# Eight chunks of the second layer's first gate part multiplied right behind the first layer's last product

## The chip, the cores and the metric

The kernel runs on one core of one Trainium2 chip. The metric is the device time of one execution in microseconds. The kernel before was run three times; its profile is that of one further execution. Engine names: PE is TensorE, DVE is VectorE, ACT is ScalarE, POOL is GpSimd, SP is SyncE.

## The reference

One inference step of a trunk of two layers over 128 context tokens and 128 latent tokens, width 2048, in fp32. Cut to what matters here:

```
for l in range(2):
    mod = silu(c) @ w_mod[l] + b_mod[l]            # 2048 x 6144 per layer, two conditioning vectors
    shift, scale, gate = split(mod, 3)
    h = rms_norm(x, norm_w[l]) * (1 + scale) + shift
    columns = h @ w_in[l]                          # q, i, ff, fb, g, attention, S5, merge gates
    o_hg = hgrn2_both_directions(...)              # gated linear recurrence, 8 heads
    o_at = attention(...)
    o_s5 = s5_both_directions(...)                 # complex diagonal scan, then GLU
    merged = g_hg*(o_hg @ w_br[0]) + g_at*(o_at @ w_br[1]) + g_s5*(o_s5 @ w_br[2])
    x = x + gate * (merged @ w_out[l])
y = rms_norm(x, final_norm)
```

The modulation vector is computed in six parts of 1024 columns for each layer. Parts 0 to 3 hold shift and scale, parts 4 and 5 the gate, which is needed only at the very end of its layer.

## The kernel before

**The products.** Every large product goes through `gemm` (line 160): an output group is 512 columns wide, for both token sets (s = 0, 1), so it holds two banks of the PSUM pool `pg` (four banks). A weight piece `raw` (256 rows by 512 columns, 512 KB) is loaded by SP; ACT rounds each half of it to `wh` (line 138), DVE forms the remainder `wl` (line 139), and TensorE does six matmuls for a half: lines 178, 179 and 180 for each s. `raw`, `wh` and `wl` have four buffers each. A `in_group` or `w_out` group is 16 halves, 96 products; a `w_br` group is 8 halves, 48 products. There are 8064 such products, 4032 in each layer. In layer two the product numbered 5760 from the program's start is the last one of the first merge gate, and the next one is the first of the first branch's `w_br`, which multiplies `oh` and `ol`, the transposed output of the HGRN mixer.

**The side work.** `mod_part` (line 245) is a generator that loads 128 x 2048 chunks `wm` of `w_mod` (1 MB each, 256 rows of it), multiplies them by the conditioning vectors, 16 matmuls of 32 x 256 for each two chunks ("a burst"; the profile counts 32 rows for it), and adds the bias `bm`. Its `plan` names the PSUM pool, how many chunks accumulate in one bank, and how many make a burst. The parts of the gate use pool `m`: before the change the plan is `("m", 2, 2)` four times, so a bank is taken for one burst and given back after its `tensor_add`. `side_work` (line 141) advances the generator at a given rate at each weight piece; in layer one the parts 4 and 5 of layer one and 0 to 3 of layer two run there, in layer two the generator `gates` with layer two's parts 4 and 5.

**The small matmuls.** Pool `m` (`pm`, line 73, two banks of 128 x 512) also serves everything that the mixers need between the products: `transpose4` (tiles `tr`), the attention's `trq`, `trk`, `sc`, `ao`, and the HGRN unit's `lv`, `o`, `kt`, `st`. Pool `b` (two banks) serves the S5 mixer (`bt`, `cb`, `bu`, `yp`).

**The HGRN unit** (`hgrn_unit`, line 449) runs for each token set and each half of the heads, the two token sets in turn. It goes through seven levels. At each one ACT copies `mix` (line 488), TensorE multiplies `lv` into a bank of pool `m` (line 492), DVE merges the bank into `A` by a predicated copy (line 494), and DVE multiplies `Z` by decay factors (line 508, twice). After the seven levels comes `o` (lines 525 to 528), its norm (lines 530 to 536 and `rstd`), for s = 0 also `kt`, `kts`, `st`, `sts` (lines 540 to 550), then the product with the SiLU gate (line 1003) and the transposes for the branch.

**The S5 scan** (lines 889 to 895) is a loop of 64 steps of four small DVE operations for each quarter of the groups; it has lower priority on DVE than the HGRN unit.

**The end of a layer** (from line 1071): four groups of `w_out`; after the fourth DVE forms x, ACT its squares, `token_rstd` the norm, then `normed` (line 371) scales x into `xn` (line 382), TensorE transposes it, and DVE and ACT form `hf`, `hh`, `hl`, the left factors of the next layer.

**What sets the order.** A scheduler with priorities writes the instruction order of each engine when the kernel is built; on the chip each engine then executes its list in order. A matmul in TensorE's list that waits holds up every one behind it.

Of the kernel before, what the change touches and what calls it, by code (L numbers as in the profile page):

```python
# [22 lines left out]
L = 2  # L23
# [5 lines left out]
MB = 2  # L29
# [4 lines left out]
MTAGS = ((("k4", "q4"), 1), (("k4", "q4"), 1), (("k4", "k4"), 1))  # L34
# [20 lines left out]
P_PE = 6_000_000  # L55
# [6 lines left out]
class Builder:  # L62
# [74 lines left out]
    def split_from(self, src, hi, lo):  # L137
        self.nc.scalar.copy(hi, src)  # L138
        self.nc.vector.tensor_sub(lo, src, hi.bitcast(F32))  # L139

    def side_work(self):
        if self.side is not None:
            self.side_credit += self.side_rate
            while self.side_credit >= 1:
                self.side_credit -= 1
                if next(self.side, None) is None:
                    self.side = None
                    break
# [7 lines left out]
    def start_side(self, gen, rate):  # L156
        self.finish_side()
        self.side, self.side_rate, self.side_credit = gen, rate, 0.0

    def gemm(self, pieces, hi, lo, nk):  # L160

        nc = self.nc
        ps = [self.pg.tile([128, 512], F32, tag="g", name=self.nm("g")) for _ in range(2)]
        for kk, src in enumerate(pieces):
            self.side_work()
            with self.prio(P_TOP):
                raw = self.wp.tile([128, 2, 512], F32, tag="raw", name=self.nm("raw"), bufs=RAW)
                nc.sync.dma_start(raw, src.rearrange("p (a b) -> p a b", a=2))
            for j in range(2):
                with self.prio(P_TOP):  # L170
                    wh = self.wp.tile([128, 512], F32R, tag="wh", name=self.nm("wh"))
                    wl = self.wp.tile([128, 512], F32R, tag="wl", name=self.nm("wl"))
                    self.split_from(raw[:, j], wh, wl)
                k = 2 * kk + j
                with self.prio(P_PE):
                    for s in range(2):
                        sl = slice(s * 128, s * 128 + 128)
                        nc.tensor.matmul(ps[s], lo(k)[:, sl], wh, start=(k == 0), stop=False)  # L178
                        nc.tensor.matmul(ps[s], hi(k)[:, sl], wh, start=False, stop=False)  # L179
                        nc.tensor.matmul(ps[s], hi(k)[:, sl], wl, start=False, stop=(k == nk - 1))  # L180
        return ps

    def rstd(self, ssq, n, width):
# [61 lines left out]
    def mod_part(self, l, part, prio, tags, plan):  # L245
# [5 lines left out]
        nc, io = self.nc, self.io  # L251
# [4 lines left out]
        kb = 0  # L256
        for bank, run, burst in plan:
            apart = burst > 1
            ps = None
            for k0 in range(kb, kb + run, burst):  # L260
                ws = []
                for k in range(k0, k0 + burst):
                    with self.prio(P_TOP):
                        tag, n = next(tags)
                        for i in range(0, 2, n):
                            w = self.t(tag if isinstance(tag, str) else tag[i], "wm", (128, n * 1024))
                            nc.sync.dma_start(w, io["w_mod"][l, part, k][:, i * 1024:(i + n) * 1024])
                            ws += [w[:, j * 1024:(j + 1) * 1024] for j in range(n)]
                    if apart:
                        yield True  # L270
                with self.prio(prio):
                    if ps is None:
                        pool = dict(g=self.pg, m=self.pm, b=self.pb)[bank]
                        ps = pool.tile([128, 512], F32, tag=bank, name=self.nm("mod"))
                    for j, k in enumerate(reversed(range(2 * k0, 2 * (k0 + burst)))):
                        for i in range(4):
                            with self.prio(P_MIX if j + i else prio):
                                nc.tensor.matmul(ps[32 * i:32 * i + 32, 0:256], self.cT[:, 2 * k:2 * k + 32],  # L278
                                                 ws[k - 2 * k0][:, i * 256:i * 256 + 256], start=(k0 == kb and j == 0),
                                                 stop=(k0 + burst == kb + run and j == 2 * burst - 1),  # L280
                                                 tile_position=(0, 32 * i))
                    if k0 + burst == kb + run:
                        nc.vector.tensor_add(bm, bm, ps[:, 0:256])
                if k0 + burst < 8:
                    yield True
            kb += run
# [634 lines left out]
    def layer(self, l, x, rs):  # L921
# [144 lines left out]
        if l + 1 == L:  # L1066
            fn = self.t("ys", "fn", (128, D))
            src = io["final_norm"]
            with self.prio(P_PREP):
                nc.gpsimd.dma_start(fn, bass.AP(src.tensor, src.offset, [[0, 128], [1, D]]))  # L1070
        for n in range(4):
            ps = self.gemm([io["w_out"][l, n, kk] for kk in range(8)],
                           lambda k: mt[2 * (k // 8)][:, k % 8], lambda k: mt[2 * (k // 8) + 1][:, k % 8], 16)
            sl = slice(n * 512, n * 512 + 512)
            if n == 3:
                self.finish_side()
                with self.prio(P_CHAIN):
                    nc.scalar.activation(self.ts("warm", (128, 1)), self.eye32[:, 0:1], AF.Sqrt)
            for s in range(2):
                with self.prio(P_LAST if n == 3 else P_TOP):  # L1080
                    gb = self.t2("gb")
                    nc.gpsimd.dma_start(gb, bass.AP(self.gate_d.tensor, self.gate_d.offset + (l * 2 + s) * D + n * 512,
                                                    [[0, 128], [1, 512]]))
                    xr = self.t2("xr")
                    nc.gpsimd.dma_start(xr, (io["x"] if l == 0 else self.x_d)[s][:, sl])
                    nc.vector.tensor_mul(gb, gb, ps[s])
                    nc.vector.tensor_add(xn[s][:, sl], gb, xr)
                    if l + 1 < L:
                        nc.gpsimd.dma_start(self.x_d[s][:, sl], xn[s][:, sl])
                    self.square(ssq, xn, s, n)  # L1090
                if l + 1 == L:
                    with self.prio(P_TOP + 500_000):
                        nc.vector.tensor_mul(xn[s][:, sl], xn[s][:, sl], fn[:, sl])
# [49 lines left out]
    def build(self):  # L1143
# [19 lines left out]
            pass  # L1163
        with self.prio(P_PREP):
            self.setup()
        for l in range(L):
            x, rs = self.layer(l, x, rs)
            if l + 1 < L:
                def gates():
                    tags = itertools.cycle(MTAGS)  # L1170
                    for p in (4, 5):
                        yield from self.mod_part(L - 1, p, P_PE, tags, [("m", MB, MB)] * (8 // MB))

                self.gates = gates()
        with self.prio(P_TOP):
            self.final(x, rs)

# [106 lines left out]
```

## Time and profile before

| | |
|---|---|
| runs (us) | 2308.33, 2309.62, 2308.81; median 2308.81 |
| profiled execution | 2313.16 us, span 2311.1 us |
| PE | 2252.0 us busy, 97% of the span, 13320 instructions |
| DVE | 1817.3 us busy, 79% |
| ACT | 1191.2 us busy, 52% |
| mean granted TensorE clock | 0.992 |
| chain that ended last | PE 84%, DVE 3%, DMA 3% |

The share of an engine is the union of its instructions over the span. PE's rows overlap their neighbours, since matmuls are pipelined: the rate is read from the distance between starts, and a wait from the idle time in brackets behind a row.

### The profile page before, as it was taken

How to read it: one execution, taken by the hardware profiler on the slowest of the kernel's cores; microseconds unless marked ns; L12 is line 12 of the kernel's file. 1: busy time of each engine (PE TensorE's matmuls, PEld its weight loads, DVE VectorE, ACT ScalarE, POOL GpSimd, SP SyncE). 2: the span in 40 equal slices, each digit the busy share in tenths (PEclk: the TensorE clock that was granted, in tenths of full speed). 3: DMA queues.
4: the chain of work that ended last, by engine and by line, in shares of the span. 5: the costliest groups of instructions: out<-in, count | busy, mean ns of one | idle time of the engine just before them, and what ended most of it. 6: DMA issues, size and time to landing. Idle time of an engine off the chain costs nothing.

```text
span 2311.1 us, 38488 instructions
## 1 busy us (share of the span) xinstructions
PE 2252.0 (97%) x13320; PEld 1818.5 (79%) x13320; DVE 1817.3 (79%) x4863; ACT 1191.2 (52%) x2064; POOL 133.8 (6%) x245
## 2 busy tenths in 40 slices
PE   6999999999999999999989999999999999999997
PEld 4668888888887777877767888888888877888886
DVE  4987799889869779875575898899959958956565
ACT  4436655555454354544447565555564544555454
POOL 2000000100100100000010001000010010000000
PEclk8999999999999999999999999999999999999999
DMA  9975454345548869588764554344546667656765
GB/s 377 362 288 170 145 181 155 123 134 195 186 159 282 316 212 326 198 274 284 270 233 137 177 175 151 127 166 152 190 148 196 200 207 266 200 175 224 241 202 171
DMA packets 131363, 483.87 MB, mean 209 GB/s; under 512 B 17200, under 2 KB 17808, under 8 KB 126688
## 3 DMA queue, kind: packets, MB, share of 16 engines
q1 hardware_dynamic: 120960, 456.38, 58.0%
q0 software_dynamic: 9488, 23.97, 3.4%
q8 instruction: 104, 1.70, 0.3%
q10 hardware_dynamic: 720, 1.07, 0.1%
q14 instruction: 91, 0.75, 0.1%
HBM read 474.36 MB, written 6.98 MB: 208 GB/s over the span
## 4 chain that ended last, share of the span: by engine, by line
PE 84%; DVE 3%; DMA 3%; issue 1%; ACT 1%; POOL 0%; SPq 0%; DVEq 0%; POOLq 0%; ACTq 0%
PE g L178 24%; PE g L180 24%; PE g L179 23%; PE bu L877 3%; PE lv L492 2%; PE mod L278 2%; PE tr L134 2%; DMA wm<-w_mod 1%; PE yp L908 1%; DVE wl L139 1%; DMA bm<-b_mod 1%; DMA gate_d<-bm 1%; PE bt L795 1%; PE yp L901 1%; PE ao L632 0%
## 5 line engine op out<-in xcount | busy, mean ns | idle before, releaser
L138 ACT CAST wh<-raw 128x512 fp32r<-128x512 f32 x1344 | 828.3, 623 | 900.9 <-PE g L179 599.0
L139 DVE TENSOR_TENSOR wl<-raw,wh 128x512 fp32r<-128x512 f32 x1344 | 914.2, 687 | 285.5 <-ACT wh L138 260.1
L178 PE MATMUL g<-wh,hl 128*128 128x512 f32 x1984 | 784.4, 395 | 6.7 <-DVE hl L139 5.6
L179 PE MATMUL g<-wh,hh 128*128 128x512 f32 x1984 | 778.0, 392 | 0.0
L180 PE MATMUL g<-wl,hh 128*128 128x512 f32 x1984 | 698.7, 398 | 1.5 <-DVE wl L139 1.2
L178 PEld LDWEIGHTS g<-wh,hl 128*128 128x128 f32 x1984 | 373.6, 188 | 96.3 <-DVE hl L139 7.7
L179 PEld LDWEIGHTS g<-wh,hh 128*128 128x128 f32 x1984 | 373.7, 188 | 77.0 <-issue 1.0
L180 PEld LDWEIGHTS g<-wl,hh 128*128 128x128 f32 x1984 | 366.4, 188 | 84.0 <-DVE wl L139 4.7
L889 DVE TENSOR_TENSOR p<-s5sc,Sb 128x64 f32<-128x64 f32 x512 | 140.1, 274 | 16.8 <-ACT Sb L881 7.2
L178 PE MATMUL g<-wh,ol 128*128 128x512 f32 x384 | 151.3, 394 | 0.0
L179 PE MATMUL g<-wh,oh 128*128 128x512 f32 x384 | 150.0, 391 | 0.0
L895 DVE TENSOR_TENSOR Sb<-Sb,p 128x64 f32<-128x64 f32 x512 | 140.9, 275 | 9.0
L891 DVE TENSOR_TENSOR p<-s5sc,Sb 128x64 f32<-128x64 f32 x512 | 138.3, 270 | 0.0
L180 PE MATMUL g<-wl,oh 128*128 128x512 f32 x384 | 130.6, 394 | 0.8 <-DVE wl L139 0.8
L894 DVE TENSOR_TENSOR p<-p,p 128x64 f32<-128x64 f32 x512 | 112.7, 220 | 6.0
L179 PE MATMUL g<-wh,mt 128*128 128x512 f32 x256 | 99.8, 390 | 0.0
L178 PE MATMUL g<-wh,mt 128*128 128x512 f32 x256 | 99.6, 389 | 0.0
L278 PE MATMUL mod<-wm,cs 128*32 128x256 f32 x1408 | 90.1, 388 | 7.1 <-DMA wm<-w_mod 6.9
L178 PEld LDWEIGHTS g<-wh,ol 128*128 128x128 f32 x384 | 72.1, 188 | 16.8 <-issue 0.8
L180 PEld LDWEIGHTS g<-wl,oh 128*128 128x128 f32 x384 | 71.3, 188 | 17.7 <-DVE wl L139 2.1
L179 PEld LDWEIGHTS g<-wh,oh 128*128 128x128 f32 x384 | 72.1, 188 | 14.9
L180 PE MATMUL g<-wl,mt 128*128 128x512 f32 x256 | 83.1, 392 | 0.0
(325 smaller groups left out, 2116.7 us busy)
## 6 DMA issues: line engine op xcount, KB each, us to landing
raw<-w_in SPq DMA_DIRECT2D x496, 512.0 KB, 4.2
wm<-w_mod SPq DMA_DIRECT2D x128, 512.0 KB, 7.9
raw<-w_br SPq DMA_DIRECT2D x96, 512.0 KB, 4.2
wm<-w_mod SPq DMA_DIRECT2D x32, 1024.0 KB, 10.5
raw<-w_out SPq DMA_DIRECT2D x64, 512.0 KB, 4.4
raw<-w_glu SPq DMA_DIRECT2D x16, 512.0 KB, 4.3
gb<-gate_d POOLq DMA_DIRECT2D x16, 256.0 KB, 6.4
x<-x SPq DMA_DIRECT2D x2, 1024.0 KB, 6.9
```

Source lines behind the costliest of these rows:

```text
L134: nc.tensor.transpose(ps[:, k], src[:, k * 128:(k + 1) * 128], self.ident)
L138: self.nc.scalar.copy(hi, src)
L139: self.nc.vector.tensor_sub(lo, src, hi.bitcast(F32))
L178: nc.tensor.matmul(ps[s], lo(k)[:, sl], wh, start=(k == 0), stop=False)
L179: nc.tensor.matmul(ps[s], hi(k)[:, sl], wh, start=False, stop=False)
L180: nc.tensor.matmul(ps[s], hi(k)[:, sl], wl, start=False, stop=(k == nk - 1))
L278: nc.tensor.matmul(ps[32 * i:32 * i + 32, 0:256], self.cT[:, 2 * k:2 * k + 32], ws[k - 2 * k0][:, i * 256:i * 256 + 256], start=(k0 == kb ...
L877: nc.tensor.matmul(pps[x][:, j2, k], Bl[pr, d, ri, k, j2, :], U2[pr, j2, 2 * qh + k].rearrange("p s t -> p (s t)"), start=True, stop=True, ...
L889: tt(p0.rearrange("p d (j s) -> p d j s", s=2), view(sc, qd * 32, [[16, 2], [1, 16], [0, 2]]), view(Sb, i, [[ds, 2], [2 * W, 16], [W, 2]]) ...
L891: tt(p1, view(sc, 128 + qd * 64, [[32, 2], [16, 2], [1, 16]]), view(Sb, i + RI, [[ds, 2], [-RI, 2], [W, 16]]), ALU.mult)
L894: tt(p0, p0, p1, ALU.add)
L895: tt(cur, cur, p0, ALU.add)
```

## The change

`gates` is created once, in `build`, and layer one takes its first steps: the generator is advanced at three places of layer one's `w_out` stage, so that the first two chunks of layer two's part 4 are loaded during the third and fourth group, and four chunks (in the change's title eight, of 128 rows each) are multiplied behind the fourth group's last product. `last_product` records that product, and `behind` adds an order edge from it to each of the 32 matmuls. The rest of layer one's side work is finished before the third group and no longer before the end of the fourth. The first two chunks now take buffers `H8`, and the plan of the gate parts is `("m", 8, 2)` once: all eight chunks of a part accumulate in one bank of pool `m`.

```diff
+    def ahead(self, n):
+
+        for _ in range(n):
+            next(self.gates)
...
+    def behind(self, ins, prev):
+
+        if prev:
+            self.tc.add_manual_dep(ins.ins, prev.ins.name, mybir.DependencyInfo(
+                mybir.DependencyClass.NoSync, mybir.DependencyReason.DATA), reason="order")
+        return ins
...
-                        nc.tensor.matmul(ps[s], hi(k)[:, sl], wl, start=False, stop=(k == nk - 1))
+                        self.last_product = nc.tensor.matmul(ps[s], hi(k)[:, sl], wl, start=False, stop=(k == nk - 1))
...
         for n in range(4):
+            if n > 1 and l + 1 < L:
+                if n == 2:
+                    self.finish_side()
+                self.ahead(1)
             ps = self.gemm([io["w_out"][l, n, kk] for kk in range(8)],
...
             if n == 3:
+                if l + 1 < L:
+                    self.mod_after = self.last_product
+                    self.ahead(1)
+                    for _ in range(MB):
+                        self.ahead(1)
+                    self.ahead(1)
+                    self.mod_after = None
                 self.finish_side()
...
+        def gates():
+            tags = itertools.chain((("H8", 2), ("H8", 2)), itertools.cycle(MTAGS))
+            for p in (4, 5):
+                yield from self.mod_part(L - 1, p, P_PE, tags, [("m", 8, MB)])
...
-                        yield from self.mod_part(L - 1, p, P_PE, tags, [("m", MB, MB)] * (8 // MB))
```

**What moves on the engines.** The first place is PE's list at the end of layer one; `mod` is the modulation's bank, `wm` a chunk, `tr` the transpose of the next layer's `xn`. Before:

```order
L178 MATMUL g_12946<-wh_13113,mt_11306 128x512
L179 MATMUL g_12946<-wh_13113,mt_11305 128x512
L180 MATMUL g_12945<-wl_13114,mt_11305 128x512
L180 MATMUL g_12946<-wl_13114,mt_11305 128x512
L134 MATMUL tr_13160<-ident,xn_13158 128x128 x4
L134 MATMUL tr_13174<-ident,xn_13172 128x128 x4
L178 MATMUL g_13279<-wh_13283,hl_13157 128x512
```

Changed:

```order
L192 MATMUL g_12951<-wl_13120,mt_11305 128x512
L192 MATMUL g_12952<-wl_13120,mt_11305 128x512
L290 MATMUL mod_13129<-wm_12949,cs 32x256 x8
L290 MATMUL mod_13129<-wm_12751,cs 32x256 x8
L290 MATMUL mod_13129<-wm_13152,cs 32x256 x4
L290 MATMUL mod_13129<-wm_13150,cs 32x256 x4
L290 MATMUL mod_13129<-wm_13148,cs 32x256 x4
L290 MATMUL mod_13129<-wm_13146,cs 32x256 x4
L134 MATMUL tr_13207<-ident,xn_13205 128x128 x4
L134 MATMUL tr_13221<-ident,xn_13219 128x128 x4
```

Two bursts, 32 matmuls, now stand between layer one's last product and the first transpose of layer two. All go to one tile, `mod_13129`, whose later bursts stand behind products 6312 and 6358 of layer two; part 5's four bursts follow behind products 6396 to 6526.

The second place is PE's list in layer two, where the first gate ends and the first branch begins (behind product 5760). Before, `g_19819` being the gate and `g_20000` the branch:

```order
L180 MATMUL g_19818<-wl_19987,hh_13214 128x512
L178 MATMUL g_19819<-wh_19986,hl_13215 128x512
L179 MATMUL g_19819<-wh_19986,hh_13214 128x512
L180 MATMUL g_19819<-wl_19987,hh_13214 128x512
L178 MATMUL g_20000<-wh_20004,ol_19781 128x512
L179 MATMUL g_20000<-wh_20004,oh_19780 128x512
```

Changed, from the gate's last product on (`lv`, `o`, `kt`, `st` are HGRN's second half of the heads):

```order
L192 MATMUL g_19866<-wl_20034,hh_13261 128x512
L505 MATMUL lv_18938<-Z_18794,mix_18795 128x128 x4
L505 MATMUL lv_18948<-Z_18785,mix_18786 128x128 x4
L505 MATMUL lv_18958<-Z_18794,mix_18795 128x128 x4
L505 MATMUL lv_18968<-Z_18785,mix_18786 128x128 x4
L505 MATMUL lv_18978<-Z_18794,mix_18795 128x128 x4
L505 MATMUL lv_18988<-Z_18785,mix_18786 128x128 x4
L505 MATMUL lv_18997<-Z_18794,mix_18795 128x128 x4
L538 MATMUL o_19005<-i_18781,A_18849 128x128 x4
L555 MATMUL kt_19028<-ident,Z_18785 128x128 x4
L560 MATMUL st_19035<-i_18781,kts_19033 128x128 x4
L538 MATMUL o_19043<-i_18782,A_18857 128x128
```

Before, the last `lv` stood behind product 5476 and the last `st` and the transposes of `q` behind products 5544 to 5596, each with products in front of and behind it. Now seven `lv` of four matmuls, `o` (4 and 12), two `kt`, two `st` (4 each) and two `tr` (4 each) stand between product 5760 and product 5761 with no product among them; two more `tr` follow behind product 5772.

The third place is DVE's list in the same stretch of the changed kernel (`p` and `Sb` are the S5 scan's; `A` and `Z` the HGRN unit's):

```order
L507 COPY_PREDICATED A_18849<-msk,lv_18948 128x512
L521 TENSOR_TENSOR Z_18785<-Z_18785,T_18856 128x2x16x16 x2
L907 TENSOR_TENSOR p_3978_17047<-p_3978_17047,p_3979_17048 128x64
L908 TENSOR_TENSOR Sb_16829<-Sb_16829,p_3978_17047 128x2x32
L902 TENSOR_TENSOR p_3980_17053<-s5sc_1236,Sb_16829 128x64
L904 TENSOR_TENSOR p_3981_17054<-s5sc_1236,Sb_16829 128x64
L907 TENSOR_TENSOR p_3980_17053<-p_3980_17053,p_3981_17054 128x64
L507 COPY_PREDICATED A_18857<-msk,lv_18958 128x512
L521 TENSOR_TENSOR Z_18794<-Z_18794,T_18864 128x2x16x16 x2
L908 TENSOR_TENSOR Sb_16829<-Sb_16829,p_3980_17053 128x2x32
```

The third quarter of the S5 scan, which before began behind product 5754, has moved ahead into this stretch: DVE's list alternates between the HGRN unit's remaining levels and scan steps. From the merge of the first of the seven `lv` to the split of the first transpose for the branch (`ol`) it holds 23 scan steps, 6 further predicated copies, 14 multiplications of `Z`, 8 operations of 128 x 512 of the norms and gates, and 12 small ones.

On SP the two `H8` chunks (1 MB each) now stand behind the first `w_out` piece, four loads of 512 KB follow behind the third group's pieces, and the 4 MB are gone from layer two.

## Rows read from the trace of the kernel before

**Rows 1.** Engine windows of layer two: from HGRN's start, its middle, behind product 5760.

```profile
core 0: us, PE busy (x) PEld busy (x) DVE busy (x) ACT busy (x) POOL busy (x), PEclk, DMA share, GB/s
1418.00:1722.00 304.00, 303.68 (x1971) 256.18 (x1970) 263.15 (x688) 169.62 (x288) 21.92 (x36) 1.00 0.47 155
1480.00:1680.00 200.00, 200.00 (x1170) 170.88 (x1170) 188.58 (x520) 109.60 (x184) 7.06 (x11) 1.00 0.49 164
1722.00:1848.00 126.00, 126.00 (x568) 104.01 (x570) 118.84 (x355) 64.02 (x105) 0.00 (x0) 1.00 0.59 190
```

**Rows 2.** PE's timeline between the layers: start, length, what, count, idle before it.

```profile
1201.54 0.63 PE L180 MATMUL g<-wl,mt 128*128 128x512 f32 x2
1208.43 1.09 PE L134 MATMUL tr<-ident,xn 128*128 128x128 f32 x4 [6.27 <-DVE xn L382]
1211.47 1.09 PE L134 MATMUL tr<-ident,xn 128*128 128x128 f32 x4 [1.95 <-DVE xn L382]
...
1212.95 0.63 PE L179 MATMUL g<-wh,hh 128*128 128x512 f32 x1
1213.38 0.63 PE L180 MATMUL g<-wl,hh 128*128 128x512 f32 x1
```

**Rows 3.** Engine windows of the same stretch, for the granted clock (the column PEclk).

```profile
1202.00:1208.00 6.00, 0.17 (x1) 0.00 (x0) 4.72 (x14) 1.89 (x6) 1.10 (x2) 0.72 0.88 263
1208.00:1213.00 5.00, 2.62 (x10) 1.98 (x11) 3.14 (x8) 0.97 (x2) 0.00 (x0) 0.50 0.20 82
```

**Rows 4.** PE's timeline in layer two at one burst of the gate part.

```profile
2131.20 1.93 PE L278 MATMUL mod<-wm,cs 128*32 128x256 f32 x32
2133.06 0.73 PE L180 MATMUL g<-wl,oh 128*128 128x512 f32 x2
```

**Rows 5.** PE's timeline in HGRN's second half: `lv` in both banks, `st`, `o`, transposes.

```profile
1595.67 1.95 PE L492 MATMUL lv<-Z,mix 128*128 128x128 f32 x16
...
1645.54 1.05 PE L547 MATMUL st<-i,kts 128*128 128x128 f32 x8
1646.43 0.39 PE L525 MATMUL o<-i,A 128*128 128x128 f32 x2
...
1649.57 0.60 PE L542 MATMUL kt<-ident,Z 128*128 128x128 f32 x4
1649.93 0.49 PE L178 MATMUL g<-wh,hl 128*128 128x512 f32 x1
```

**Rows 6.** DVE's timeline in HGRN's second half: one scan step alone, then steps interleaved.

```profile
1633.05 0.28 DVE L889 TENSOR_TENSOR p<-s5sc,Sb 128x64 f32<-128x64 f32 x1
...
1633.99 0.69 DVE L139 TENSOR_TENSOR wl<-raw,wh 128x512 fp32r<-128x512 f32 x1
...
1637.60 0.27 DVE L895 TENSOR_TENSOR Sb<-Sb,p 128x64 f32<-128x64 f32 x1
1637.77 0.67 DVE L534 TENSOR_REDUCE ssq<-sq 128x4 f32<-128x512 f32 x1
1638.37 0.26 DVE L889 TENSOR_TENSOR p<-s5sc,Sb 128x64 f32<-128x64 f32 x1
...
1638.73 0.68 DVE L139 TENSOR_TENSOR wl<-raw,wh 128x512 fp32r<-128x512 f32 x1
...
1639.41 0.21 DVE L894 TENSOR_TENSOR p<-p,p 128x64 f32<-128x64 f32 x1
1639.54 0.68 DVE L139 TENSOR_TENSOR wl<-raw,wh 128x512 fp32r<-128x512 f32 x1
```

**Rows 7.** DVE's timeline at one level: predicated copy and two multiplications of `Z`.

```profile
1614.82 0.74 DVE L494 COPY_PREDICATED A<-msk,lv 128x512 f32<-128x512 uint8 x1
1615.44 1.29 DVE L508 TENSOR_TENSOR Z<-Z,T 128x512 f32<-128x512 f32 x2
```

**Rows 8.** Engine windows of layer one's last 115 us, and PE's wait there.

```profile
1088.00:1203.00 115.00, 111.83 (x581) 87.56 (x579) 69.19 (x120) 52.59 (x92) 13.14 (x22) 0.99 0.78 268
...
PE mod L278 <- DMA wm<-w_mod: 2.3, 1, 2.3
```

More of the change, by code (lines that the diff above doesn't have):

```diff
@@ L277, in mod_part @@
                             with self.prio(P_MIX if j + i else prio):
[L278 to L281, printed above, removed]
+                                self.behind(nc.tensor.matmul(
+                                    ps[32 * i:32 * i + 32, 0:256], self.cT[:, 2 * k:2 * k + 32],
+                                    ws[k - 2 * k0][:, i * 256:i * 256 + 256], start=(k0 == kb and j == 0),
+                                    stop=(k0 + burst == kb + run and j == 2 * burst - 1),
+                                    tile_position=(0, 32 * i)), self.mod_after)
                     if k0 + burst == kb + run:
@@ L1165, in build @@
             self.setup()
+        self.mod_after = None
+        def gates():
+            tags = itertools.chain((("H8", 2), ("H8", 2)), itertools.cycle(MTAGS))
+            for p in (4, 5):
+                yield from self.mod_part(L - 1, p, P_PE, tags, [("m", 8, MB)])
+        self.gates = gates()
         for l in range(L):
             x, rs = self.layer(l, x, rs)
[L1168 to L1171, printed above, removed]
-                        yield from self.mod_part(L - 1, p, P_PE, tags, [("m", MB, MB)] * (8 // MB))
-                self.gates = gates()
         with self.prio(P_TOP):
```

## The prediction

> **What bounds the kernel now.** I read the engine windows of layer two first, then TensorE's timeline between the layers, then the timelines of HGRN's second half, and against them the instruction order of both kernels. The windows [rows 1] show TensorE busy in all 126 us behind product 5760: 568 matmuls, 0.222 us each, the distance at which products follow each other at the full clock, so nothing holds TensorE there. From HGRN's start up to that product it is busy in 303.68 of 304 us, and DVE in 263.15. So a matmul taken out of this stream is worth its own time, and a matmul that fills an idle TensorE costs nothing. The one idle place of any size lies between the layers [rows 2]: behind the last product TensorE waits 6.27 us until the first transpose may start, then 1.95 us more.
>
> **What the change gains.** Two bursts leave layer two's stream. One burst takes 1.86 us there, from its start to that of the next product [rows 4], so the two are worth 3.7 us. Between the layers they need the same 3.7 us of a wait of 6.27 us whose end is set by DVE (the scaled x), so they fit, if their chunks have landed by then. A second gain comes with it: in the wait the granted clock falls, to 0.50 in the next 5 us, which is the 1.2 GHz level [rows 3]; a product then takes 0.43 us, from start to start [rows 2], and the two groups of four transposes last 1.09 us each against 0.60 us for four at 2.4 GHz [rows 2, 5]. If the bursts keep the clock up, the transposes alone give back 1.0 us and the first five products about 1 us. The engine still idles some 2.5 us behind them, so I take 1.0, with 0 and 2 as ends.
>
> **What the change costs in loads.** 4.2 MB more have to come within layer one's last 115 us. The transfers there are busy in 0.78 of the time at 268 GB/s [rows 8], that is 344 GB/s while busy, so 4.2 MB are 12.2 us and 25 us are free. But 2.5 MB of it (7.3 us) stand on SP's queue among the loads of the remaining side work, for which TensorE already waits 2.3 us once [rows 8]; behind SP's issue of the two `H8` chunks stand two `w_out` pieces and four side loads. I take 1 us, with 0 and 7.3 as ends. The two chunks in `H8` and the 1 MB pairs in the small buffers are read right behind the last product, and the second half of `hh` and `hl`, which needs the `H8` buffers next, is written more than 5 us later; I cost that at nothing. Finishing the side work at the third group moves no burst by more than 10 products; nothing. Fewer `tensor_add` of `bm` on DVE: nothing on the path.
>
> **What the change costs in PSUM.** This is the large term, and the diff hides it in the plan. With `("m", 8, 2)` the bank taken between the layers is given back only after part 4's last burst, behind product 6358. Pool `m` has two banks, so all of layer two's transposes, attention and HGRN matmuls share one. Before, the two token sets' `lv` stand side by side, 16 rows within 1.95 us [rows 5], one bank each; now each `lv` has to wait until DVE has merged the one before. The instruction order shows the result: in the changed kernel the levels of HGRN's second half come about 24 products apart for each `lv`, not for each pair, and seven of them, both `o`, both `kt`, both `st` and two transposes are left over when product 5760 is done. The next product is the first branch's, which needs the output of all of that, and TensorE keeps its order. So TensorE waits out a chain.
>
> Its length, from DVE's order between the first of these merges and the first split for the branch. Predicated copies: 6 by 0.62 us, from the start of one to that of the next operation [rows 7], 3.7. Multiplications of `Z`: 14, two in 1.29 us with a last tail of 0.08, so 0.60 each [rows 7], 8.4. Norm and gate operations: 8 by 0.60, as the reduction [rows 6], 4.8. Twelve small ones: not above the 0.17 us of the short operation in [rows 6], 2.0. Scan steps, which stand in DVE's list between them and can't be passed: 23. One alone takes 0.94 us (four operations, 1633.05 to 1633.99); interleaved with others its parts take 0.17 + 0.36 + 0.13 = 0.66 [rows 6]. That is 15.2 to 21.6 us; most steps in the list are cut by an HGRN operation, so I take 0.75 each, 17.3. Sum 36.2 us, ends 34.1 and 40.5. Ahead of it come the first `lv`, 0.9 us, and its merge, 0.6, behind it the split, 0.6: 38 us, ends 36 and 43, from product 5760 to product 5761.
>
> TensorE works in that time, and this work is no longer in the stream ahead. Four matmuls of `lv` or `st` take 0.89 us (`st` to `o` in [rows 5]); seven `lv` 6.2, two `st` 1.8, 16 of `o` at the same rate 3.6. Four transposes take 0.36 (`kt` to the product behind it, [rows 5]): two `kt` and four `tr` 2.2. Together 13.8 us, which I subtract. The clock adds something: TensorE has work in little over a third of the wait, and [rows 3] show the 1.2 GHz level after 6 us without any, so the 13.8 us may double. Only where DVE stands waiting for TensorE does that count (mainly the 12 matmuls of `o` for the latent tokens and the chain behind them); 3 us, ends 0 and 13.8.
>
> Elsewhere with one bank I count 2 us (0 to 10): the projections `i` of the second half are evacuated later, so the following gate groups find two accumulator banks instead of four and can't start before the previous group is evacuated.
>
> **The sum.** 38 - 13.8 + 3 + 2 + 1 - 3.7 - 1 = +25.5 us. On the profiled execution's 2313.16 us that is 2338.7; the median of the runs is 4.35 us (0.19%) lower, so 2334.
>
> A rule of the Trainium skill speaks against the change too, and more strongly. [Rows 7] show a merge of 0.62 us, and [rows 5] products of TensorE between the small matmuls, so a busy bank costs nothing as long as products stand behind the waiting `lv`. The Trainium skill (Perfetto Trace Analysis, Optimizing Tensor Performance, Matmuls) says that independent groups of matmuls should rotate through different banks, so that one's evacuation overlaps the next one's matmuls. By that rule alone every small group of layer two would pay, not only the ones left at the end. No run so far shows a single bank.
>
> **The rivals.**
>
> *DVE sets the pace, and the order costs nothing (not slower).* In the middle of HGRN DVE is busy in 188.58 of 200 us, and behind product 5760 in 118.84 of 126 [rows 1]. If DVE bound both stretches, it would not matter which of its work comes first: the scan steps done during the wait, and some 11 ahead of it, are missing behind product 5760, 34 by 0.75 = 25 us, and would be given back there. The result would be the gains alone, 2308.8 - 4.7 = 2304 us, or 2305 with the 1 us of the loads. It decides from the point at which DVE holds the products behind 5760 apart. Against it: they come 0.222 us apart, TensorE's own rate, so nothing can be given back there. Chance 0.10, half of it faster and half unchanged.
>
> *One bank costs everywhere (slower).* From HGRN's start each of 32 `lv` waits for a merge, 0.62 us and the way to it and back. If TensorE's order has no slack there, each exposes about 0.7 us (an estimate: the 0.62 us of [rows 7] and a tenth): 22 us more, 2356. For it: the order places each `lv` as soon as the bank is expected free. Against it: between two of them stand 24 products, 5.4 us. The page's rule above would lead here. Chance 0.13.
>
> *The loads are late, so the change does not do what it says (slower).* If the last pair of chunks lands after the last product, the burst waits on TensorE, and the transposes of layer two are queued behind it, so each microsecond counts in full; or the side work waits the whole 7.3 us earlier. Price up to 7 us, 2341. Against it: 25 us of free transfer time. Chance 0.12.
>
> *The forecast:* 0.65.
>
> **How the numbers follow.** The likeliest case gives 2334. Its low end takes the wait at 36, no cold clock, no other loss and the full gains: +16.5, less some relief of DVE ahead of product 5760 (11 scan steps come in, 8.2 us, about 19 us of HGRN go out), so 2316. Its high end takes 43 us and half of the cold clock's 13.8, and the second rival is at 2356, so 2358. That leaves out the first rival and the far tail, less than 0.2. A measurement of this kernel can tell about 0.2%, 4.6 us, from no change: faster 0.05, unchanged 0.05, slower 0.90.
>
> **What would show it.** In the changed profile: the two bursts between about 1202 and 1206 us with the first transpose not later than before; a single idle stretch of TensorE between the first gate and the first branch of layer two, with `lv` about 2.7 us apart and DVE nearly full of `Z`, `A` and scan steps; from there on the same rate as before. I am wrong if products stand between those `lv`, if the wait is below 20 us, or if the stream ahead of it shortens by much more than 13.8 us.

## The result, and the profile after

The changed kernel takes 2350.99 us (median of four runs, 2346.93 to 2351.41), the kernel before 2308.57 us in the runs beside it: a ratio of 1.0172, 95% interval 1.016 to 1.0184, or 42.4 us more. The forecast was 2334 us, slower, with a range of 2316 to 2358. Its sign was right, and so was the place of most of the loss; the loss was two thirds larger than the 25.2 us forecast (2334 less 2308.81).

The profiled execution of the changed kernel took 2351.36 us. From its page, the span and the first section (engine, busy time, share, instructions):

```profile
span 2349.6 us, 38463 instructions
...
PE 2269.6 (97%) x13320; PEld 1831.4 (78%) x13320; DVE 1822.0 (78%) x4857; ACT 1197.3 (51%) x2068; POOL 133.9 (6%) x245
```

The share of TensorE is what it was, 97%: a share over the whole span hides a wait of 2% of it, the more so since TensorE works, slowly, in most of that wait. The engine windows show it (columns as in [rows 1]). From HGRN's start to product 5760, the wait behind it, and what follows:

```profile
1416.00:1715.00 299.00, 293.66 (x1847) 244.16 (x1846) 250.87 (x674) 160.38 (x273) 20.80 (x38) 0.99 0.42 145
1722.00:1765.00 43.00, 26.89 (x114) 23.00 (x113) 39.27 (x138) 10.57 (x19) 1.60 (x2) 0.58 0.20 73
1768.00:1890.00 122.00, 120.31 (x738) 98.13 (x738) 93.33 (x251) 61.84 (x101) 7.77 (x16) 0.99 0.46 158
```

In the 43 us of the wait TensorE is busy for 26.89 us, at a mean granted clock of 0.58 against 1.00 in all three windows of [rows 1], and DVE for 39.27. TensorE's own timeline there, from the last product of the first gate (1721.22) to the first of the first branch (1765.52), for which it needs 44.30 us and needed 0.23 before:

```profile
1721.22 0.39 PE L192 MATMUL g<-wl,hh 128*128 128x512 f32 x1
1721.45 1.05 PE L505 MATMUL lv<-Z,mix 128*128 128x128 f32 x8
1724.96 1.84 PE L505 MATMUL lv<-Z,mix 128*128 128x128 f32 x8 [2.45 <-DVE A L507]
1727.71 2.04 PE L505 MATMUL lv<-Z,mix 128*128 128x128 f32 x8 [0.91 <-DVE A L507]
1730.72 2.05 PE L505 MATMUL lv<-Z,mix 128*128 128x128 f32 x8 [0.96 <-DVE A L507]
...
1743.26 2.08 PE L538 MATMUL o<-i,A 128*128 128x128 f32 x8 [0.82 <-DVE A L507]
1746.87 1.11 PE L555 MATMUL kt<-ident,Z 128*128 128x128 f32 x4 [1.53 <-ACT sq L545]
...
1764.75 1.12 PE L134 MATMUL tr<-ident,q 128*128 128x128 f32 x4 [1.40 <-DVE ol L139]
1765.52 0.78 PE L190 MATMUL g<-wh,ol 128*128 128x512 f32 x1
```

The seven `lv` come some 3 us apart, with no product between them. Eight rows of `lv` last 1.05 us at the start of the wait, as in [rows 5] (16 in 1.95), and from the third on 2.04: TensorE has fallen to its 1.2 GHz level. Between the layers, the two early bursts (64 rows) stand where [rows 2] have idle time:

```profile
1200.71 0.62 PE L192 MATMUL g<-wl,mt 128*128 128x512 f32 x2
1201.26 3.66 PE L290 MATMUL mod<-wm,cs 128*32 128x256 f32 x64
1207.64 0.63 PE L134 MATMUL tr<-ident,xn 128*128 128x128 f32 x4 [2.71 <-DVE xn L395]
1210.12 1.11 PE L134 MATMUL tr<-ident,xn 128*128 128x128 f32 x4 [1.86 <-DVE xn L395]
```

The second group of transposes starts 9.41 us behind the start of the last products' row, against 9.93 before (1211.47 less 1201.54, [rows 2]). The bursts are free, as the change intends.

The starts of the products divide the execution into stretches. This table, from the traces of both kernels, is the measure for all that follows (us from the start of one product to that of the other; 4032 is layer one's last product, 5760 the last of the first gate):

| stretch | before | after | difference |
|---|---|---|---|
| to product 4032 | 1201.8 | 1200.9 | -0.9 |
| 4032 to 4033, between the layers | 10.59 | 10.16 | -0.4 |
| 4033 to 5521 | 437.57 | 420.75 | -16.8 |
| 5521 to 5665 | 43.59 | 64.13 | +20.5 |
| 5665 to 5760 | 32.59 | 25.24 | -7.4 |
| 5760 to 5761, the wait | 0.23 | 44.30 | +44.1 |
| 5761 to 5809 | 10.89 | 15.87 | +5.0 |
| 5809 to 8064, the rest | 559.45 | 554.00 | -5.5 |

The sum is 38.6 us, the difference of the two spans 38.5. The medians are 42.4 apart, since the profiled execution of before was 4.6 us above its median and that of after only 0.4.

Until product 5760 a part of HGRN's work has gone out of the stream, worth 14.8 us at the rates of before (each kind of TensorE's instructions counted, at its mean time from its start to the next start). Yet only 3.6 us are saved there, so 11.2 us are lost. A stretch's difference is not its loss, since work has also moved between stretches: from 5521 to 5665, some 12 of the 20.5 us are work that stood in the stretches beside it before, levels of HGRN and input of the S5 scan's third quarter, and some 8.5 us are lost. Most of that loss is at this input. TensorE's timeline there:

```profile
1653.74 0.60 PE L808 MATMUL bt<-ident,Sb 128*128 128x128 f32 x4
1657.13 1.97 PE L808 MATMUL bt<-ident,Sb 128*128 128x128 f32 x8 [2.79 <-ACT Bl L809]
1659.03 1.18 PE L816 MATMUL cb<-C,Sb 128*32 128x32 f32 x64
1660.14 1.23 PE L890 MATMUL bu<-U,Bl 64*128 64x128 f32 x8
```

and ACT's, where `U` and `g` are other work, and `Bl` is what `bt` waits for:

```profile
1646.71 5.29 ACT L854 COPY U<-uT 32x512 f32<-32x512 f32 x8
1652.03 2.18 ACT L138 CAST wh<-raw 128x512 fp32r<-128x512 f32 x4
1654.22 1.28 ACT L459 ACT_TABLE_LOAD   x1
1655.52 1.08 ACT L459 ACTIVATE g<-g 128x512 f32<-128x512 f32 x2
1656.49 1.08 ACT L809 COPY Bl<-bt 128x512 f32<-128x512 f32 x2
```

Three of the four `bt` stand behind one another with no product between, and ACT reaches `Bl` late. The clock falls as well (0.82 from 1652 to 1661.3 us): eight rows of `bt` last 1.97 us. Before, the first two stood side by side, with their `Bl` ahead of ACT's `g` and products between them and the third (TensorE's timeline, with one row of ACT's):

```profile
1687.48 1.03 PE L795 MATMUL bt<-ident,Sb 128*128 128x128 f32 x8
1690.73 1.06 ACT L796 COPY Bl<-bt 128x512 f32<-128x512 f32 x2
1693.98 0.60 PE L795 MATMUL bt<-ident,Sb 128*128 128x128 f32 x4
1694.88 0.60 PE L795 MATMUL bt<-ident,Sb 128*128 128x128 f32 x4
```

All `bt` together take 5.5 us more than before from start to start up to product 5760, half of the 11.2 us. The rest is spread: `o` 1.5 us, `yp` 1.1, the products 1.0, no other kind more than 0.8.

### The profile page after: what moved, and what is told of

It reads as the page before. It is cut to its first block, busy times and chain, and to the rows that moved or that the text cites. A ratio compares the mean times of both kernels' runs of the same rounds, so it can differ in the third digit from the quotient of the medians.

```text
span 2349.6 us, 38463 instructions
## 1 busy us (share of the span) xinstructions
PE 2269.6 (97%) x13320; PEld 1831.4 (78%) x13320; DVE 1822.0 (78%) x4857; ACT 1197.3 (51%) x2068; POOL 133.9 (6%) x245
## 5 line engine op out<-in xcount | busy, mean ns | idle before, releaser
L190 PEld LDWEIGHTS g<-wh,ol 128*128 128x128 f32 x384 | 72.7, 189 | 16.8 <-ACT wh L138 0.8
```

## The experiments

Ten kernels: `return_bank`, `no_edges`, `hold_g` and `two_runs` beside the same runs of before (median 2311.68), `hold_only`, `filled` and `scan_behind` beside 2310.37, `hold_attn`, `filled_scan` and `fill_gap` beside 2310.23. All ratios are to before.

**The bank given back after each burst** (`return_bank`), an edit to the changed kernel:

```
-                yield from self.mod_part(L - 1, p, P_PE, tags, [("m", 8, MB)])
+                yield from self.mod_part(L - 1, p, P_PE, tags, [("m", MB, MB)] * (8 // MB))
```

> The early bursts stay, with their loads and order edges, but the plan is ("m", 2, 2) four times again, so the bank of pool m is given back after each burst. Theory A (the loss is the held bank): the instruction order of HGRN is that of before, no wait behind product 5760, and the gains of the change are left: the gap 1.3 us shorter, two bursts (3.8 us) out of layer two. 2308.6 - 5 = 2303.5 us, between 2301 and 2306. Rival B (the early loads and bursts, or the side work that ends at the third group, upset layer two): 2340 to 2351 us.

Measured: 2304.98 us, ratio 0.9969 (0.9957 to 0.9981). Theory A. With the same early loads, bursts and edges, the wait is gone. The engine window behind product 5760 reads as the third of [rows 1]:

```profile
1722.00:1848.00 126.00, 126.00 (x585) 103.55 (x584) 119.23 (x356) 62.42 (x104) 1.92 (x4) 1.00 0.61 195
```

By the stretches of layer two, the gain is in the last one: 554.58 us from 5809 to 8064, 4.9 less than before. That number is good to some 2 us only: `no_edges` and `fill_gap` below, with the same order there, take 556.66 and 552.84. The gap, expected 1.3 us shorter, is not (10.65).

**The bank held, and nothing else** (`hold_only`), an edit to the kernel before, with `behind` and `last_product` taken over from the change:

```
             if n == 3:
+                if l + 1 < L:
+                    with self.prio(P_PE):
+                        self.held = self.pm.tile([128, 512], F32, tag="m", name=self.nm("held"))
+                        self.behind(nc.tensor.transpose(self.held[:, 0:128], self.ident, self.ident), self.last_product)
...
+                    if ps is None and (l, part) == (L - 1, 4):
+                        ps = self.held
...
-                        yield from self.mod_part(L - 1, p, P_PE, tags, [("m", MB, MB)] * (8 // MB))
+                        yield from self.mod_part(L - 1, p, P_PE, tags, [("m", 8, MB)])
```

> The kernel before, with one edit: a bank of pool m is taken behind layer one's last product (one transpose of the identity is written into it) and given back when part 4 of layer two's gate, which accumulates in it, is done. No chunk is loaded or multiplied early. Theory A (the held bank is the whole loss): seven lv and what follows stand between products 5760 and 5761 as in the change, a wait of about 44 us, and the two bursts and the longer gap come back: 2351 + 3.8 + 1.3 = 2356 us, 2350 to 2361. Rival B (early loads and bursts): 2309 us.

Measured: 2357.55 us, ratio 1.0213 (1.0196 to 1.0231). Theory A again: no chunk is early, and all of the loss is there, with 43.83 us from product 5760 to 5761 and 65.86 from 5521 to 5665. The two kernels together show that the held bank is the cause, of the wait and of the loss ahead of it, and that the bursts and loads are not.

**A bank of another pool held** (`hold_g`), an edit to the changed kernel:

```
-                yield from self.mod_part(L - 1, p, P_PE, tags, [("m", 8, MB)])
+                yield from self.mod_part(L - 1, p, P_PE, tags, [("g", 8, MB)])
```

> As the change, but the bank that is held for all of part 4 comes from the products' pool g (plan ("g", 8, 2)), which leaves three of its four banks. Theory A: HGRN's order is that of before and nothing waits behind product 5760. Each of some 18 groups in that time must wait for the eviction of one bank of the group ahead; three products (0.67 us) stand ahead of that wait, so 0.3 to 1.3 us each, 5 to 23 us: 2308.6 - 5 + 13 = 2316 us, 2304 to 2327. Rival B (bursts and loads are the cause): about 2350 us or more.

Measured: 2306.1 us, ratio 0.9976 (0.9965 to 0.9986), near the low end. From product 4033 to 5521 it takes 442.32 us, 4.7 more than before: for 15.5 groups at most 0.3 us each, since 1.3 us of it are `st` and `tr` that moved into the stretch. So it is not holding a bank that is dear, but holding one of a pool of two on which a chain runs.

**The bank given back behind the attention** (`hold_attn`), an edit to `hold_only`, whose plan is that of before again:

```
+            if l + 1 == L:
+                nc.vector.tensor_add(self.ts("end", (128, 1)), self.held[:, 0:1], og_at[1][:, 1023:1024])
+                self.held = None
...
-                    if ps is None and (l, part) == (L - 1, 4):
-                        ps = self.held
```

> hold_only, but the bank is given back behind the attention's last operation in layer two, before HGRN's levels begin. The order then has HGRN's first lv behind product 4960 (before: 4895), its last behind 5560 (before: 5476) and the last st behind 5622; nothing is left over at product 5760. Theory A (a held bank costs only from the point at which the work that it delays is what the next product needs): within 3 us of the kernel before, 2307 to 2313. Rival (one bank costs at every small group that has to wait for it; the attention and 20 transposes of layer two go through one bank): 5 to 20 us more than before, 2315 to 2330.

Measured: 2318.63 us, ratio 1.0033 (1.0021 to 1.0045), 8.4 us above the median of before (7.6 by the ratio). The time is in the rival's range, but neither theory is right as it stood. There is no wait at product 5760 (0.23 us), so the large loss does come only where work is left over. But the time is not that of before: from product 4033 to 5809 the kernel takes 9.1 us more for the same work. Two stretches are longer mainly because work moved into them: 5521 to 5665 takes 50.49 us (+6.9, of which 6.5 are HGRN's end), and 5761 to 5809 takes 14.33 (+3.4, of which 2.8 are `bu` and `yp`). The loss lies ahead of 5521 (4.4 us) and from 5665 to 5760 (3.6); by kind, 6.4 us of the 9.1 are at the products and 1.8 at `bt`. TensorE's waits from 1600 to 1800 us name DVE (line waited for: total, times, longest):

```profile
PE g L186 <- DVE wl L139: 2.8, 2, 1.7
PE bt L801 <- ACT Bl L802: 0.3, 1, 0.3
```

and DVE waits for ACT there, between HGRN's last products with the gate (`q`):

```profile
1696.94 0.69 DVE L139 TENSOR_TENSOR wl<-raw,wh 128x512 fp32r<-128x512 f32 x1 [1.65 <-ACT wh L138]
1698.85 0.69 DVE L1012 TENSOR_TENSOR q<-q,g 128x512 f32<-128x512 f32 x1 [1.22 <-ACT g L452]
```

ACT's list from 1694 to 1701 us holds, beside the `wh`, two loads of activation tables, `g`, `ys` and the first of the S5 input's `uT` and `U`. So the products' own factors come late here, ahead of any bank wait. That the delay pushed two busy stretches of the other engines onto each other is the likely reason, but no run shows it apart.

**TensorE kept busy in the wait** (`filled`), an edit to `hold_only`; `fill` is called behind the last seven `lv`, both `kt` and both `st`:

```
+    def fill(self, ins, n):
+
+        for _ in range(n):
+            ins = self.behind(self.nc.tensor.transpose(self.held[:, 256:384], self.ident, self.ident), ins)
...
+            if l + 1 == L and hf == 1 and 2 * i + s > 6:
+                self.fill(lv, 8)
...
+                if l + 1 == L and hf == 1:
+                    self.fill(lv, 8)
```

> hold_only with 88 more transposes on TensorE in the wait, eight (0.7 us at full clock) behind each of the seven lv, both kt and both st, into unused columns of the held bank; their results are not used. Theory C (the wait is a round trip of TensorE and DVE through one bank, and TensorE's part of it runs at the 1.2 GHz level): the fillers keep the clock up in the wait, a lv of eight rows takes 1.05 us and not 2.04, and the wait is 30 to 38 us instead of 44: 6 to 14 us less than hold_only. Rival D (the sum of the prediction: DVE's list sets the wait): the wait stays at 42 us or more, and the time is that of hold_only or up to 8 us more.

Measured: 2349.45 us, ratio 1.0168 (1.0153 to 1.0183), 8.1 us less than `hold_only`, whose interval lies above. The wait falls from 43.83 to 35.37 us, 2.6 us of it in the seven `lv` and 5.8 in the `o`, `kt`, `st` and `tr` behind the last of them. More work on TensorE made the kernel faster. Its timeline in the wait:

```profile
1728.21 1.13 PE L505 MATMUL lv<-Z,mix 128*128 128x128 f32 x8 [0.36 <-DVE A L509]
1729.17 1.04 PE L460 MATMUL held<-ident 128*128 128x128 f32 x8
1730.26 1.13 PE L505 MATMUL lv<-Z,mix 128*128 128x128 f32 x8
1731.22 1.04 PE L460 MATMUL held<-ident 128*128 128x128 f32 x8
```

and the engine window of most of it, `hold_only`'s first:

```profile
1724.00:1764.00 40.00, 26.16 (x113) 22.53 (x112) 34.71 (x123) 8.80 (x15) 1.59 (x2) 0.57 0.18 66
1726.00:1757.00 31.00, 24.65 (x188) 22.45 (x188) 28.65 (x97) 8.73 (x15) 1.59 (x2) 0.94 0.24 82
```

The granted clock is 0.94 for 0.57, and most of the late `lv` are 2.05 us apart for 2.95.

**No scan step in the wait** (`scan_behind`), an edit to the changed kernel; `units_end` is the HGRN unit's last operation on DVE:

```
+        if (l, hh) == (L - 1, 1):
+            return uT, U2
...
-                tt(p0.rearrange("p d (j s) -> p d j s", s=2), view(sc, qd * 32, [[16, 2], [1, 16], [0, 2]]),
-                   view(Sb, i, [[ds, 2], [2 * W, 16], [W, 2]]), ALU.mult)
+                self.behind(tt(p0.rearrange("p d (j s) -> p d j s", s=2),
+                               view(sc, qd * 32, [[16, 2], [1, 16], [0, 2]]),
+                               view(Sb, i, [[ds, 2], [2 * W, 16], [W, 2]]), ALU.mult),
+                            self.units_end if (l, qd, i) == (L - 1, 2, 0) else None)
...
-                u_half(1)
+                late = u_half(1)
+            elif l + 1 == L:
+                for qh in range(2):
+                    self.s5_quarter(l, 1, qh, *late, ys)
```

> The change, with the third quarter's S5 scan put behind the last HGRN operation on DVE by an order edge, so that no scan step stands in DVE's list between the seven lv. Theory C (round trip through one bank, TensorE at the 1.2 GHz level): the lv stay about 3 us apart, the wait stays at 38 us or more while DVE is busy in little over half of it, and the time is within 5 us of the change: 2346 to 2356. Rival D (DVE's list sets the wait, 23 steps of 0.75 us are 17 of it): the wait falls to 27 us and the time to 2334.

Measured: 2350.29 us, ratio 1.0173 (1.0158 to 1.0188): no different from the change. The wait is 43.21 us. The engine windows of the wait and of what follows:

```profile
1724.00:1763.00 39.00, 25.84 (x108) 22.00 (x108) 21.29 (x52) 8.69 (x15) 1.59 (x2) 0.54 0.18 66
1763.00:1890.00 127.00, 125.60 (x660) 102.65 (x659) 115.56 (x349) 60.74 (x99) 4.79 (x7) 0.98 0.53 173
```

DVE's busy time in the wait has fallen to 21.29 us of 39, and next to nothing came of it: the wait is 1.1 us shorter. Its timeline tells why:

```profile
1727.91 0.72 DVE L507 COPY_PREDICATED A<-msk,lv 128x512 f32<-128x512 uint8 x1 [1.05 <-PE lv L505]
1728.53 1.28 DVE L521 TENSOR_TENSOR Z<-Z,T 128x512 f32<-128x512 f32 x2
1730.86 0.72 DVE L507 COPY_PREDICATED A<-msk,lv 128x512 f32<-128x512 uint8 x1 [1.05 <-PE lv L505]
```

With the steps gone, DVE stands 1.05 us for TensorE at a level; with them, it filled that hole. Most merges are 2.95 us apart here, as in `hold_only`, which keeps the steps (2.7 to 3.6 in the change): some 2.1 from the start of an `lv` at the 1.2 GHz level to its merge, and 0.9 from the merge to the next `lv`. The scan steps taken out come behind product 5760 and cost nothing there either (5809 to 8064 takes 554.23 us, in the change 554.00).

**Both together** (`filled_scan`): `hold_only` with the two edits above, and `fill(lv, 6)` for 8.

> hold_only with fillers as in filled, six for eight (0.5 us each time), and the third quarter's S5 scan behind the last HGRN operation on DVE as in scan_behind. Theory C (round trip: lv 1.05 us, the way to DVE, a merge of 0.6, the way back): with the clock up and the fillers shorter, a lv comes 1.8 to 2.05 us behind the one before, and the wait is 32 to 36 us, since scan steps fill only holes of the round trip: within 3 us of filled, 2346 to 2353. Rival D (once the clock is up DVE's list, 23 scan steps of 0.75 us in it, is what sets the wait of filled): the wait falls to some 20 us and the time to 2335.

Measured: 2344.12 us, ratio 1.0146 (1.013 to 1.0162). The wait is 32.15 us, at the low end of theory C's range, and the time is 2 us below it. The rival's 20 us are far. With the clock up, the scan steps and the two fillers fewer are worth 3.2 us of the wait, 0.9 of it in the seven `lv` and 2.4 behind the last; which of the two it is stays open.

**Without the order edges** (`no_edges`), an edit to `return_bank`:

```
-        if prev:
+        if False:
```

> As return_bank, without the order edges: the bursts then stand behind products 3810 and 3834, in the middle of the last w_out group. Theory A: a burst in a stream that keeps TensorE busy costs its 1.9 us wherever it stands, so 3.8 us come into layer one and 3.8 us leave layer two, and the gap is as before: 2308.6 us, 2306 to 2312, the upper end if the chunks are not there 50 us earlier and TensorE waits for them. Rival: the place behind the last product is not what gains, then it is as fast as return_bank.

Measured: 2308.39 us, ratio 0.999 (0.9981 to 1.0). As expected: moved from one busy stream into another, the bursts gain nothing or a little. About half of what `return_bank` gains comes from the edges (3.4 of 6.7 us between the medians), and the two intervals just touch, so the share is rough.

**Two accumulations of four chunks** (`two_runs`), the changed kernel with the plan `[("m", 4, MB)] * 2`:

> As the change, but four of the eight chunks accumulate in one bank, twice (plan ("m", 4, 2) twice): the bank is held over the gap between the layers only. Theory A: as return_bank, 2303.5 us, 2301 to 2306; one addition of the bias tile fewer per part does not show. Rival B: 2340 us or more. If a bank held over the gap costs something by itself, it is over 2306.

Measured: 2306.28 us, ratio 0.9971 (0.996 to 0.9982), as `return_bank`; the median is 0.3 us over the bound set, beside runs of before that are 3 us over the 2308.6 it was set from. Held over the gap alone, a bank costs nothing that shows.

**The gap filled as well** (`fill_gap`), an edit to `return_bank`:

```
+                    ps2 = self.psm("fill", (128, 512))
+                    with self.prio(P_PE):
+                        for _ in range(24):
+                            self.behind(nc.tensor.transpose(ps2[:, 0:128], self.ident, self.ident), self.mod_after)
```

> return_bank with 24 more transposes of the identity (2.2 us at full clock) behind the two early bursts in the gap between the layers; their results are not used. If the clock of the layer's start is what the early bursts could not keep up: the two groups of transposes take 0.60 us each and the first five products 0.22 us, and from layer one's last product to layer two's first it is 9.5 to 10.2 us instead of 10.65: 0.5 to 2 us less than return_bank, 2303 to 2305. Rival: DVE's chain of the normed x sets both waits and the clock at the first products is low all the same: no difference, 2305.

Measured: 2304.66 us, ratio 0.9975 (0.9964 to 0.9985): no difference from `return_bank` that can be measured. In the trace the transposes behind the gap last 0.62 us and not 1.09, and the gap is 10.15 us for 10.65. So the clock is worth 0.5 us here, and DVE's `xn` sets the rest. The fillers are not needed for it: the change, `two_runs` and `hold_g` have the first transposes at 0.63 us and the gap at 10.15 or 10.16 without them.

## Why the forecast was right, and where it was short

The forecast was +25.5 us between profiled executions; the traces show +38.6. That 2350.99 us lies in the range is owed in part to its wide upper end, which stood for a longer wait, a colder clock and the second rival, and not for a loss of this size ahead of the wait. By its terms:

| term | forecast | measured |
|---|---|---|
| the wait, with its clock | 38 + 3 | +44.1 |
| work gone from the stream ahead, less what one bank costs there | -13.8 + 2 | -3.6 |
| 5761 to 5809 | 0 | +5.0 |
| layer one, loads | +1 | -0.9 |
| the gap's clock | -1 | -0.4 |
| two bursts, and the rest behind | -3.7 | -5.5 |

- **The cause** was right: the bank that the plan holds. `hold_only` has it alone and the whole loss, `return_bank` everything else and none of it.
- **The step that failed most** is "Elsewhere with one bank I count 2 us (0 to 10)". The HGRN work that left the stream between 4033 and 5760 is worth 14.8 us at the rates of before (13.8 in the forecast, which counts four `tr`; six have left, one of which stood behind product 5686). The stream got only 3.6 shorter, so 11.2 us were lost in it. The reason given, that gate groups wait for accumulators, is not what the trace shows there: one such wait of 1.3 us on the eviction of a group stands in TensorE's waits before 1715 us, beside the 2.79 us of `bt` above. Half of the loss is `bt` at the S5 input, which met the delayed HGRN work; `hold_attn` loses 9.1 us in the stream without any wait at 5760, but there mainly at products whose factors come late. What brings each part of it about was not separated further. The 5.0 us behind the wait were left out: three `tr` (2.8 us, 1.4 of it a wait for DVE's `ol`), and the first nine products at the 1.2 GHz level.
- **The wait** was near in size (38 + 3 against 44.1) and wrong in its working. The forecast added up DVE's list, with 17.3 us of scan steps, and counted the clock "only where DVE stands waiting for TensorE". The runs turn that round: without scan steps the wait stays at 43.2 us, and with the clock up it falls by 8.5. It is a round trip of TensorE, DVE and ACT through one bank, with TensorE's part at the 1.2 GHz level for most of it: 19 us for the seven `lv`, 25 from the last of them to product 5761. The scan steps filled its holes. The sum of DVE's list came out right by luck: the list just about filled a wait that something else had set. DVE being busy for 39.27 of 43 us looked like the proof, and was not. Two readings behind it were too simple: of the 14 pairs of `lv` in before, five stand side by side as in [rows 5], the others 2 to 19 products apart, and four of the list's 14 multiplications of `Z` are of half the size (two in 0.76 us in `scan_behind`), which is 1 us less than counted.
- **The clock** term was 3 us with ends 0 and 13.8; `filled` gives back 8.5 of the wait and 8.1 of the time. The Trainium skill (Perfetto Trace Analysis, Matmul Optimizations) says that TensorE's power follows its use and that matmuls should run back to back in batches; this trace agrees, with 0.57 and 0.94 for the same `lv` alone and with fillers.
- **The first rival** (DVE paces both stretches) falls: behind the wait the stream is as long whether the third quarter's scan ran ahead (554.00 us) or not (554.23 in `scan_behind`, 554.58 in `return_bank`), and in `hold_only`, where it ran ahead and no burst is gone, it is not shorter than before (561.39 against 559.45).
- **The second** (each `lv` pays) falls as it was worked out. In the changed kernel the `lv` that stand in the stream, most of them some 24 products apart, cost next to nothing: all levels' `lv` take 16.1 us more than before, and the seven of the wait account for 15.6 of it. The Trainium skill's rule of rotating banks (Perfetto Trace Analysis, Optimizing Tensor Performance, Matmuls) describes the wait, where nothing stood between the groups, and not the stream, where products covered the merge.
- **The third** (late loads) did not come: TensorE's waits for `w_mod` in layer one's last 120 us were 2.9 us, against 2.3 in [rows 8].
- **The gains** were right: the bursts fit into the gap without delaying it, and `return_bank` keeps them, at 0.9969 (6.7 us between the medians, for 4.7 forecast). How much of that are the two bursts is known only roughly: the last stretch is 2.8 to 6.6 us shorter than before in kernels with the same order there.

## What to carry to other kernels

Here a buffer lent out of a pool cost nothing where it was lent, and showed up where the pool's other users ran late. Before a plan holds one, list who else takes from that pool, follow the delayed work in the instruction order up to its first consumer, and look for what is left over there. Give it back at each burst, or take it from the pool whose users have cover (here three of four accumulators did, at 0.3 us a group). Where work moves between stretches, compare them for the same work, not by their times alone. When an engine looks full during a wait, ask whether its work set the length or merely filled it, and price TensorE's part of a round trip at its low clock.

## What was not expected of the hardware

- Useless matmuls made the kernel faster: 88 transposes more, 8.1 us less, since the same eight rows of `lv` last 1.13 us and not 2.04. In the changed kernel TensorE is busy for 26.89 of 43 us of that wait, and its granted clock is 0.58 all the same.
- Layer one, whose work hardly differs between these kernels, ends between 1195.7 and 1203.0 us in the profiled executions (start of product 4032). A difference of a few us between two single executions, the -0.9 us of the loads above among them, says nothing by itself. In layer two, 4033 to 5521 repeats within 0.6 us in the five kernels with before's order there (437.39 to 438.00), but 5809 to 8064 only within 3.8 us in three of the same order (552.84 to 556.66).
